# Strassen products for the gate and the first feed-forward matrix, and a feed-forward middle in quarters

## The chip, the cores and the metric

The kernel runs on one core of one Trainium2 chip. The metric is device time in microseconds (us) of one launch. TensorE (PE in the profile) multiplies, VectorE (DVE) and ScalarE (ACT) do elementwise work, GpSimd (POOL) helps with it, and SyncE (SP) issues the DMAs. TensorE's weight loads are listed apart as PEld.

## The reference

Two decoder layers over 512 tokens with 1024 features, all float32. Each layer mixes the tokens (layer 0: a gated linear recurrence and a sparse attention; layer 1: a latent attention), norms, and then runs the part that is changed here:

```
h = layer_norm(DN_ALPHA * x + m, ln1_g[i], ln1_b[i])
f = jnp.square(jax.nn.relu(h @ mlp_w1[i])) @ mlp_w2[i]
e = jax.nn.sigmoid(h @ ple_w_gate[i]) * (p[i] @ ple_w_proj[i])
x = layer_norm(DN_ALPHA * h + f + e, ln2_g[i], ln2_b[i])
```

`mlp_w1` is 1024 x 4096, `mlp_w2` 4096 x 1024, `ple_w_gate` 1024 x 1024, `ple_w_proj` 256 x 1024.

## The kernel before

Features lie on partitions, tokens along the free dimension, so an activation of 1024 features is eight tiles of 128 x 512 (`y[0]` to `y[7]` hold the residual stream). Every float32 factor is split into a high part (rounded to the matmul's format, by ScalarE) and a low part (what is left, by VectorE), and each product is three matmuls: high by high, high by low, low by high (`mm3`, lines 106 to 108).

Weights come in chunks of 1 MB (128 x 2048): 256 output features (two tiles n) by eight row tiles k. `wload` (lines 91 to 102) has SyncE fetch one into `wraw` (two buffers), ScalarE makes `whi` and VectorE `wlo` from it in two pieces of 1024 columns. `gemm_t` (lines 113 to 157) then runs 2 x 8 x 3 = 48 matmuls of 512 columns for a chunk. Where its input or its result is passed on by halves of the tokens, it runs 96 of 256 columns instead: for the first two chunks of the gate (`lead`), and for the last group of the second feed-forward matrix (`tail`).

In each layer the order is: output projection of the mixer, the first norm (class `Norm`, lines 200 to 323), `embed` (p by `w_proj`, 48 matmuls), the gate (4 chunks), and twice a half of the feed-forward part: 8 chunks of `mlp_w1` (in the text FF1), then 8 of `mlp_w2` (FF2, four groups of two chunks). The first norm works by halves of the tokens: sums over partitions by a matmul (line 255), subtraction and squares, the deviation by two more small matmuls (lines 268 and 282), then for each of the eight tiles a scaling on VectorE (line 313), the high part on ScalarE (line 321), the low part on VectorE (line 322) and the scaled residual on GpSimd (line 323). The gate's first two chunks start with the first half of the tokens while the second half is still being normed.

The order of the instructions on each engine is decided by a scheduler when the program is built, by priorities and by the buffers that are free; each engine then runs its list strictly in that order and waits on semaphores. A helper raises the priority of a weight's splitting by `ahead`. Matmul results go to 8 PSUM banks, of which six are taken in turn outside the attention.

Products are called 1 to 7 by their place in the changed code below; the names in the changed program are `xb` (the seven combined activations), `ws` (sums of weight blocks), `w..hi`/`w..lo` (their high and low parts), `u` and `c` (partial results), `n_t` and `n_h` (the norm's temporaries).

Of the kernel before, what the change touches and what calls it, by code (L numbers as in the profile page):

```python
# [52 lines left out]
def hybrid_kernel(ctx: ExitStack, tc: tile.TileContext, a: dict, out: bass.AP):  # L53
# [37 lines left out]
    def wload(dram, idx, n=2048, pieces=2, sub=None, raw=None, ahead=30):  # L91
        """A chunk of a weight (n columns), as high and low parts."""
        hi = wp.tile([P, 2048], F32R, tag="whi", name=nm("whi"))
        lo = wp.tile([P, 2048], F32R, tag="wlo", name=nm("wlo"))
# [105 lines left out]
    class Norm:  # L200
        """LayerNorm over the features (partitions and tiles) of y. The second norm of a layer
        takes mean and variance in one pass, with y centred first on the mean of tiles 0-3, so
        that the variance doesn't cancel; the first one takes the mean, then the variance."""
# [83 lines left out]
        def last(self, cs, rstd):  # L287
            """The end of the kernel: the tensor engine, free by now, takes the mean off."""
# [11 lines left out]
        def apply(self, cs):  # L300
# [111 lines left out]
    class Pair:  # L412
        """The outputs of two heads, as high and low parts in mixed[k]."""
# [14 lines left out]
    # ================= layer 0: RG-LRU and sparse attention =================  # L428
    def mixer0(mixed):
        with pool("m0", 1) as m0, pool("m0s") as sc:  # L430
# [14 lines left out]
            def key_halves(kx, kh, ps, j):  # L445
                """kx: low parts, high parts; kh: high parts on partitions 0-63."""
# [39 lines left out]
            # indexer scores of query blocks 1-3 (block 0 has no more keys than are selected)  # L486
# [21 lines left out]
            def topk():  # L508
                """16 rounds of 8, a round for all the blocks at a time."""
# [13 lines left out]
            # softplus(-lambda) by the atanh series of log1p, exact to float32  # L523
# [33 lines left out]
            # gates: sigmoid(z) = (1 + tanh(z / 2)) / 2; rg keeps the tanh, ix (1 + tanh) times  # L557
            # the convolved input
            def ev1(n, ps, cs):
# [7 lines left out]
                xh, xl = q1[:, n], q1[:, 4 + n]     # free until the queries come  # L567
# [51 lines left out]
            # distances for ALiBi beside the high parts of q and k  # L619
# [45 lines left out]
    def out_proj(dram, idxs, xs, norm, **kw):  # L665
# [8 lines left out]
        # the first two tiles in banks that the end of the attention leaves free  # L674
# [3 lines left out]
    # ================= MLP and per-layer embedding =================  # L678
    def embed(layer, mp):
        """p @ w_proj / 2, kept for the gate."""  # L680
        pr, pp = [], []
        for k in range(2):
            raw = mp.tile([P, S], F32, tag="sg", name=nm("praw"))
# [6 lines left out]
        def ev(n, ps, cs):  # L690
            t = mp.tile([P, S], F32, tag=f"ah{n + 2}", bufs=1, name=nm("pp"))
# [6 lines left out]
    def mlp(layer, h, pp, mp, norm):  # L698
        # sigmoid(z) = (1 + tanh(z / 2)) / 2
        def evg(n, ps, cs):  # L700
            sg = mp.tile([P, S], F32, tag="sg", name=nm("sg"))[:, cs]
            nc.scalar.activation(sg, ps[:, cs], AF.Tanh, scale=0.5)
            nc.vector.scalar_tensor_tensor(sg, sg, 1.0, pp[n][:, cs], op0=OP.add, op1=OP.mult)
            nc.vector.tensor_add(y[n][:, cs], y[n][:, cs], sg)

        gemm_t(a["w_gate"], [[layer * 4 + g] for g in range(4)], h, evg, lead=8, halves=("lead",))
        for half in range(2):
            act = [None] * 16

            def ev1(n, ps, cs):  # L710
                r = mp.tile([P, S], F32, tag="r", name=nm("r"))
                nc.scalar.activation(r, ps, AF.Relu)  # L712
                nc.scalar.activation(r, r, AF.Square)  # L713
# [345 lines left out]
```

## Time and profile before

| | us |
|---|---|
| median of 3 runs | 1299.29 |
| lowest, highest | 1299.01, 1301.18 |
| span of the profiled execution, first to last instruction | 1298.1 |
| TensorE busy in the span | 1254.7 |
| VectorE busy | 740.1 |
| ScalarE busy | 575.7 |
| GpSimd busy | 212.1 |

The profile is of one execution. The time of a run also counts what lies around the span; the median of the runs stands 1.2 us above the span of the profiled execution, whose own run time is not listed apart. A matmul's time in the profile is its latency, longer than its place in the stream: how fast TensorE goes is read from one start to the next. The two feed-forward stages lie at about 282 to 635 us (layer 0) and 933 to 1286 us (layer 1).

### The profile page before, as it was taken

What the parts mean: (1) busy time and instruction counts of PE and PEld (TensorE: products, weight loads), DVE (VectorE), ACT (ScalarE), POOL (GpSimd) and SP (SyncE); (2) the same over time, 40 slices, a digit from 0 to 9 for tenths busy, and PEclk for the clock granted to TensorE, in tenths of its full rate; (3) what the DMA queues carried; (4) which work ended last, traced back from release to release, by engine and by line L of the source; (5) the groups of instructions that cost most, each with busy time, mean ns of one, the idle gap of its engine ahead of it and who ended that gap; (6) DMA issues with size and microseconds to landing.
All of it is one profiled execution on the core that took longest, in us unless ns stands there. A gap on an engine that the chain in (4) does not pass through costs nothing.

```text
span 1298.1 us, 16201 instructions
## 1 busy us (share of the span) xinstructions
PE 1254.7 (97%) x6248; PEld 1049.7 (81%) x6248; DVE 740.1 (57%) x1437; ACT 575.7 (44%) x1066; POOL 212.1 (16%) x237
## 2 busy tenths in 40 slices
PE   7997889999999999999899999999999999999998
PEld 5685678988888888888887788799888888888888
DVE  5799978854432244336728898677544322344264
ACT  4465775533321133313356998635333211333132
POOL 1457550300000000000543443103000000000000
PEclk9798899999999999999898999999999999999999
DMA  6211120132222222222112100122322222222211
GB/s 212 97 66 65 66 81 34 66 130 97 98 98 97 98 98 97 97 97 86 49 65 98 33 33 28 55 77 87 127 98 97 98 95 95 92 96 94 98 49 66
DMA packets 20910, 110.81 MB, mean 85 GB/s; under 512 B 2464, under 2 KB 6560, under 8 KB 8640
## 3 DMA queue, kind: packets, MB, share of 16 engines
q1 hardware_dynamic: 20736, 109.18, 24.8%
q8 instruction: 49, 0.80, 0.3%
q0 software_dynamic: 96, 0.59, 0.2%
q14 instruction: 29, 0.24, 0.1%
HBM read 107.66 MB, written 2.10 MB: 85 GB/s over the span
## 4 chain that ended last, share of the span: by engine, by line
PE 81%; DVE 11%; ACT 6%; issue 1%; DMA 0%; POOL 0%; SPq 0%; ACTq 0%; DVEq 0%; POOLq 0%
PE ps L108 24%; PE ps L106 24%; PE ps L107 24%; ACT l L357 2%; DVE mb L517 2%; DVE m L516 1%; PE ps L370 1%; PE ps L751 1%; PE ps L749 1%; PE ps L750 1%; ACT whi L88 1%; DVE l L352 1%; PE ps L390 1%; DVE wlo L89 1%; DVE hl L322 1%
## 5 line engine op out<-in xcount | busy, mean ns | idle before, releaser
L88 ACT CAST whi<-wraw 128x1024 fp32r<-128x1024 f32 (+3 forms) x226 | 205.3, 936 | 399.3 <-PE ps L107 389.3
L106 PE MATMUL ps<-hh,whi 128*128 128x512 f32 (+1 forms) x1008 | 372.0, 371 | 10.3 <-ACT hh L88 6.6
L108 PE MATMUL ps<-hh,wlo 128*128 128x512 f32 (+1 forms) x1008 | 370.8, 370 | 7.9 <-POOL wlo L89 6.0
L107 PE MATMUL ps<-hl,whi 128*128 128x512 f32 (+1 forms) x1008 | 371.9, 370 | 1.2 <-POOL hl L89 1.2
L89 DVE TENSOR_TENSOR wlo<-wraw,whi 128x1024 fp32r<-128x1024 f32 (+1 forms) x172 | 194.1, 1147 | 250.0 <-ACT whi L88 249.9
L106 PEld LDWEIGHTS ps<-hh,whi 128*128 128x128 f32 x1008 | 191.7, 191 | 44.0 <-ACT hh L88 7.2
L108 PEld LDWEIGHTS ps<-hh,wlo 128*128 128x128 f32 x1008 | 191.4, 190 | 40.4 <-POOL wlo L89 6.7
L107 PEld LDWEIGHTS ps<-hl,whi 128*128 128x128 f32 x1008 | 192.0, 191 | 34.3 <-POOL hl L89 2.9
L107 PE MATMUL ps<-al,whi 128*128 128x512 f32 (+1 forms) x576 | 211.3, 367 | 0.0
L106 PE MATMUL ps<-ah,whi 128*128 128x512 f32 (+1 forms) x576 | 211.1, 367 | 0.0
L108 PE MATMUL ps<-ah,wlo 128*128 128x512 f32 (+1 forms) x576 | 210.5, 365 | 0.0
L107 PEld LDWEIGHTS ps<-al,whi 128*128 128x128 f32 x576 | 108.6, 189 | 17.9 <-issue 0.5
L108 PEld LDWEIGHTS ps<-ah,wlo 128*128 128x128 f32 x576 | 108.6, 189 | 17.9 <-issue 0.5
L106 PEld LDWEIGHTS ps<-ah,whi 128*128 128x128 f32 x576 | 108.6, 189 | 17.6
L323 POOL TENSOR_SCALAR y<-y,small 128x256 f32<-128x256 f32 x48 | 32.0, 678 | 492.1 <-DVE hl L322 492.1
L89 POOL TENSOR_TENSOR wlo<-wraw,whi 128x512 fp32r<-128x512 f32 (+2 forms) x54 | 91.8, 1718 | 79.1 <-ACT whi L88 79.1
L723 DVE TENSOR_TENSOR y<-y,ps 128x512 f32<-128x512 f32 (+1 forms) x36 | 22.6, 627 | 107.2 <-PE ps L108 107.2
L712 ACT ACTIVATE r<-ps 128x512 f32<-128x512 f32 x64 | 38.0, 594 | 88.0 <-PE ps L108 88.0
L361 POOL TENSOR_SCALAR l<-l,sums 128x512 f32<-128x512 f32 (+1 forms) x96 | 53.8, 578 | 98.8 <-DVE sums L359 69.6
L88 DVE CAST ah<-r 128x512 fp32r<-128x512 f32 x64 | 27.1, 423 | 71.9 <-ACT r L713 71.9
L357 ACT ACTIVATE l<-l,mx 128x512 f32<-128x512 f32 (+1 forms) x96 | 52.9, 553 | 11.8 <-DVE mx L355 11.3
L89 DVE TENSOR_TENSOR al<-r,ah 128x512 fp32r<-128x512 f32 x64 | 44.3, 693 | 2.2
(289 smaller groups left out, 1575.4 us busy)
## 6 DMA issues: line engine op xcount, KB each, us to landing
wraw<-in_mlp_w SPq DMA_DIRECT2D x64, 1024.0 KB, 4.8
wraw<-in_w_out SPq DMA_DIRECT2D x8, 1024.0 KB, 4.8
wraw<-in_w_gate SPq DMA_DIRECT2D x8, 1024.0 KB, 6.2
wraw<-in_w_in SPq DMA_DIRECT2D x6, 1024.0 KB, 4.8
wraw<-in_w_ukv SPq DMA_DIRECT2D x4, 1024.0 KB, 4.7
wraw<-in_w_in SPq DMA_DIRECT2D x16, 128.0 KB, 4.0
y<-in_xT SPq DMA_DIRECT2D x8, 256.0 KB, 4.2
wraw<-in_w_proj SPq DMA_DIRECT2D x2, 1024.0 KB, 5.8
```

Source lines behind the costliest of these rows:

```text
L88: (act or nc.scalar.copy)(hi, src)
L89: (sub or nc.vector.tensor_sub)(lo, src, f(hi))
L106: nc.tensor.matmul(ps, whi, xhi, start=start, stop=False)
L107: nc.tensor.matmul(ps, whi, xlo, start=False, stop=False)
L108: nc.tensor.matmul(ps, wlo, xhi, start=False, stop=stop)
L322: nc.vector.scalar_tensor_tensor(lo, yk, b, f(hi), op0=OP.add, op1=OP.subtract)
L323: nc.gpsimd.tensor_scalar(yk, yk, b, ALPHA, op0=OP.add, op1=OP.mult)
L357: nc.scalar.activation(L[blk], L[blk], AF.Exp, bias=mx[:, NB + blk:NB + blk + 1], scale=self.scale, accum_out=sums[:, blk:blk + 1])
L361: nc.gpsimd.tensor_scalar(L[blk], L[blk], sums[:, blk:blk + 1], 1.0, op0=OP.mult, op1=OP.mult)
L517: nc.vector.match_replace(out=w, in_to_replace=m8, in_values=src, imm_value=LOWEST)
L712: nc.scalar.activation(r, ps, AF.Relu)
L723: nc.vector.tensor_add(y[n][:, cs], y[n][:, cs], ps[:, cs])
```

## The change

The gate and FF1 take a chunk of weights as a 2 x 2 block matrix: columns in two tiles of 128, rows in two halves of four tiles. The normed activation is a 2 x 2 block matrix too: features in two halves of four tiles, tokens in two halves of 256. A Strassen scheme (Winograd's form) gets the four result blocks from seven block products in place of eight. Each is 4 x 3 = 12 matmuls of 256 columns.

For each chunk `front` makes the four weight sums S1 to S4 and the parts for the first four products, `back` those for the other three; the results are added up on VectorE (`u`, `c`). The first norm no longer makes high and low parts of the eight tiles; its new method `blocks` makes the seven activation blocks. Four of them (T1 to T4) need both halves of the tokens. The feed-forward part runs in four quarters of 4 + 4 chunks; the tail of FF2 is one chunk. A third pair of weight buffers is added in a pool `third`, the copy of the squared activation goes from VectorE to ScalarE, and the gate no longer starts by halves.

```diff
+        def blocks(self, cs, rstd):
...
+            for k in range(KT):
...
+                nc.vector.scalar_tensor_tensor(yk, yk, g, rstd, op0=OP.mult, op1=OP.mult)
+                if not half:
+                    put(k // 4, k % 4, yk, b)
+                elif k >= 4:
+                    put(2, k - 4, yk, b)
+                nc.scalar.activation(hk, yk, AF.Identity, bias=b)
+                nc.gpsimd.tensor_scalar(yk, hk, ALPHA, 0.0, op0=OP.mult, op1=OP.add)
+            if half:
+                for k in range(4):
...
+                    nc.vector.tensor_sub(t[0], b12, b11)
+                    nc.vector.tensor_sub(t[1], b22, t[0])
+                    nc.vector.tensor_sub(t[2], b22, b12)
+                    nc.vector.tensor_sub(t[3], b21, t[1])
+                    for i in (1, 2, 0, 3):
+                        put(3 + i, k, t[i])
...
+        def front(idx):
...
+            with tc.high_priority(120):
+                sp(t, 0, Q, a11)
+                nc.vector.tensor_add(s1, a21, a22)
+                nc.vector.tensor_sub(s2, s1, a11)
+                sp(t, Q, Q, s2)
+                nc.vector.tensor_sub(s3, a11, a21)
+                nc.vector.tensor_sub(s4, a12, s2)
+                sp(t, 2 * Q, 2 * Q, st[:, Q:3 * Q])
+            return t, raw, s4
...
+        def back(raw, s4):
...
+                sp(t, 0, 2 * Q, raw[:, 2 * Q:])
+                sp(t, 2 * Q, Q, s4)
...
+        for g, idx in enumerate(idxs):
+            x, raw, s4 = front(idx)
+            a = ps_tile()
+            product(a, x, 0, 0)
...
+            nc.scalar.copy(p1, a[:, :H])
+            b = ps_tile()
+            product(b, x, 4, Q)
...
+            nc.vector.tensor_add(u, b[:, :H], p1)
+            c = ps_tile()
+            product(c, x, 5, 2 * Q)
...
+            nc.vector.tensor_add(u3, c[:, :H], u)
+            d = ps_tile()
+            product(d, x, 3, 3 * Q)
...
+            nc.vector.tensor_add(t[:, 3 * H:], d[:, :H], u3)
+            w2 = back(raw, s4)
+            product(a, w2, 1, 0, 2 * P, False)
+            product(c, w2, 6, P, 2 * P, False)
+            nc.vector.tensor_add(t[:, 2 * H:3 * H], c[:, :H], u)
+            product(d, w2, 2, 2 * Q, start=False)
+            nc.vector.tensor_add(t[:, H:2 * H], d[:, :H], u)
+            evac(g, a[:, :H], t)
...
-        gemm_t(a["w_gate"], [[layer * 4 + g] for g in range(4)], h, evg, lead=8, halves=("lead",))
-        for half in range(2):
...
+        seven(a["w_gate"], [layer * 4 + g for g in range(4)], xb, mp, evg, third=third)
+        for part in range(4):
...
+            seven(a["mlp_w1"], [layer * 16 + part * 4 + g for g in range(4)], xb, mp, ev1, third=third)
...
-            gemm_t(a["mlp_w2"], [[b + 2 * g, b + 2 * g + 1] for g in range(4)], act, ev2, tail=half)
...
+            gemm_t(a["mlp_w2"], [[b + 2 * g] for g in range(4)], act, ev2, tail=part == 3)
```

How the program's lists change is shown at three places. On TensorE in layer 0, around the statistics of the second half of the tokens (line 255 before; lines 269 and 283 of the changed kernel), before:

```order
L106 MATMUL ps_2295<-hh_2003,whi_2275 128x256
L106 MATMUL ps_2299<-hh_1997,whi_2283 128x256
L255 MATMUL ps_2104<-n_s_326_1880,cst 128x256
L107 MATMUL ps_2299<-hl_1998,whi_2283 128x256
L106 MATMUL ps_2303<-hh_1997,whi_2283 128x256
L107 MATMUL ps_2303<-hl_1998,whi_2283 128x256
L107 MATMUL ps_2295<-hl_2004,whi_2275 128x256
L108 MATMUL ps_2295<-hh_2003,wlo_2276 128x256
L106 MATMUL ps_2291<-hh_2009,whi_2275 128x256
```

and of the changed kernel (`xb_2005` and `xb_2029` to `xb_2041` are blocks of the first half of the tokens, `xb_2199` and `xb_2202` the first tiles of T2 and T3; a row with x2 is two matmuls):

```order
L269 MATMUL ps_2144<-cst,n_s_327_1881 128x1 x2
L283 MATMUL ps_2152<-cst,n_d_2148 128x128 x2
L786 MATMUL ps_2510<-xb_2005,wh_2497 128x256
L786 MATMUL ps_2385<-xb_2029,whi_2445 128x256 x2
L786 MATMUL ps_2385<-xb_2029,wlo_2446 128x256
L786 MATMUL ps_2385<-xb_2035,whi_2445 128x256 x2
L786 MATMUL ps_2385<-xb_2035,wlo_2446 128x256
L786 MATMUL ps_2385<-xb_2041,whi_2445 128x256 x2
L786 MATMUL ps_2385<-xb_2041,wlo_2446 128x256
L786 MATMUL ps_2400<-xb_2199,whi_2372 128x256 x2
L786 MATMUL ps_2415<-xb_2202,whi_2372 128x256
L786 MATMUL ps_2400<-xb_2199,wlo_2373 128x256
```

Before, the gate's matmuls with the first half of the tokens stand around the statistics and behind them; in the changed list 12 + 1 + 9 matmuls of the gate need the first half alone (12 of them stand ahead of line 269), and the next ones read T2 and T3.

On VectorE in layer 0, at the end of the second half's norm, before (line 322 makes low parts of the normed tiles, lines 703 and 704 take up the gate's results):

```order
L322 SCALAR_TENSOR_TENSOR hl_2028<-y_72,small,hh_2027 128x256
L322 SCALAR_TENSOR_TENSOR hl_2034<-y_73,small,hh_2033 128x256
L313 SCALAR_TENSOR_TENSOR y_74<-y_74,small,ps_2144 128x256
L703 SCALAR_TENSOR_TENSOR sg_2382<-sg_2382,pp_2206 128x256
L703 SCALAR_TENSOR_TENSOR sg_2389<-sg_2389,pp_2215 128x256
L322 SCALAR_TENSOR_TENSOR hl_2040<-y_74,small,hh_2039 128x256
L704 TENSOR_TENSOR y_67<-y_67,sg_2382 128x256
```

and of the changed kernel (lines 357 to 364 make T1 to T4, line 342 their low parts, lines 765 to 769 the weight sums of the gate's first chunk, line 752 low parts of weights):

```order
L364 TENSOR_TENSOR n_t_410_2254<-n_h_354_2003,n_t_408_2252 128x256
L342 TENSOR_TENSOR xb_2259<-n_t_408_2252,xb_2259 128x256
L342 TENSOR_TENSOR xb_2262<-n_t_409_2253,xb_2262 128x256
L342 TENSOR_TENSOR xb_2268<-n_t_410_2254,xb_2268 128x256
L765 TENSOR_TENSOR ws_2374<-wraw_2370 128x512
L768 TENSOR_TENSOR ws_2374<-wraw_2370 128x512
L766 TENSOR_TENSOR ws_2374<-ws_2374,wraw_2370 128x512
L752 TENSOR_TENSOR wl_2498<-wraw_2495,wh_2497 128x512
L769 TENSOR_TENSOR ws_2374<-wraw_2370,ws_2374 128x512
L752 TENSOR_TENSOR wlo_2373<-ws_2374,whi_2372 128x512
L752 TENSOR_TENSOR wlo_2373<-ws_2374,whi_2372 128x1024
```

All sixteen T tiles and their low parts stand ahead of the first weight sum, and the low part of S2, which the second product reads, is the sixth behind the last T.

On VectorE in a chunk of FF1, before (low parts of the next chunk's weights, two copies and two low parts of the activation for each chunk):

```order
L89 TENSOR_TENSOR wlo_2872<-wraw_2873,whi_2871 128x1024 x2
L88 CAST ah_2795<-r_2792 128x512
L89 TENSOR_TENSOR al_2796<-r_2792,ah_2795 128x512
L88 CAST ah_2835<-r_2832 128x512
L89 TENSOR_TENSOR al_2836<-r_2832,ah_2835 128x512
```

and of the changed kernel (lines 809, 813 and 815 add up results of one chunk, the others prepare weights of later ones):

```order
L809 TENSOR_TENSOR c_3703<-ps_3690,u_597_3688 128x256
L752 TENSOR_TENSOR wlo_3836<-wraw_3760,whi_3835 128x1024
L752 TENSOR_TENSOR wlo_3836<-ws_3764,whi_3835 128x512
L765 TENSOR_TENSOR ws_3894<-wraw_3890 128x512
L813 TENSOR_TENSOR c_3703<-ps_3675,u_595_3673 128x256
L766 TENSOR_TENSOR ws_3894<-ws_3894,wraw_3890 128x512
L768 TENSOR_TENSOR ws_3894<-wraw_3890 128x512
L752 TENSOR_TENSOR wl_3893<-wraw_3890,wh_3892 128x512
L752 TENSOR_TENSOR wl_3893<-ws_3894,wh_3892 128x512
L769 TENSOR_TENSOR ws_3894<-wraw_3890,ws_3894 128x512
L752 TENSOR_TENSOR wl_3893<-ws_3894,wh_3892 128x1024
L815 TENSOR_TENSOR c_3703<-ps_3690,u_595_3673 128x256
```

VectorE's list for a chunk grows from six instructions to sixteen, and additions that free a PSUM bank stand between the preparations of later weights.

## Rows read from the trace of the kernel before

**Rows 1.** The page: span, busy time of the engines, chain of waits by engine.

```profile
span 1298.1 us, 16201 instructions
...
PE 1254.7 (97%) x6248; PEld 1049.7 (81%) x6248; DVE 740.1 (57%) x1437; ACT 575.7 (44%) x1066; POOL 212.1 (16%) x237
...
PE 81%; DVE 11%; ACT 6%; issue 1%; DMA 0%; POOL 0%; SPq 0%; ACTq 0%; DVEq 0%; POOLq 0%
```

**Rows 2.** Windows, a feed-forward stretch: busy us of PE, PEld, DVE, ACT, POOL, clock.

```profile
300.00:400.00 100.00, 100.00 (x443) 82.81 (x442) 38.10 (x48) 32.47 (x44) 0.00 (x0) 1.00 0.29 98
```

**Rows 3.** Timeline, PE: start, us, operation; widths 512, then 256.

```profile
600.00 0.39 PE L106 MATMUL ps<-ah,whi 128*128 128x512 f32 x1
...
608.84 0.39 PE L106 MATMUL ps<-ah,whi 128*128 128x512 f32 x1
...
609.52 0.28 PE L106 MATMUL ps<-ah,whi 128*128 128x256 f32 x1
...
615.88 0.28 PE L108 MATMUL ps<-ah,wlo 128*128 128x256 f32 x1
```

**Rows 4.** Instructions by line and form, DVE and ACT: count, busy us, mean ns.

```profile
L89 DVE TENSOR_TENSOR wlo<-wraw,whi 128x1024 fp32r<-128x1024 f32 x156 | 187.9, 1222 | 244.0 <-ACT whi L88 244.0
L88 ACT CAST whi<-wraw 128x1024 fp32r<-128x1024 f32 x178 | 182.7, 1048 | 391.9 <-PE ps L107 388.0 <-issue 3.8
...
L89 DVE TENSOR_TENSOR al<-r,ah 128x512 fp32r<-128x512 f32 x64 | 44.3, 693 | 2.2
L713 ACT ACTIVATE r<-r 128x512 f32<-128x512 f32 x64 | 40.4, 631 | 1.0
...
L313 DVE SCALAR_TENSOR_TENSOR y<-y,small,ps 128x256 f32<-128x256 f32 x56 | 24.1, 474 | 2.7 <-PE ps L282 2.6
...
L257 DVE TENSOR_TENSOR y<-y,ps 128x256 f32<-128x256 f32 x32 | 12.2, 412 | 0.9 <-PE ps L255 0.8
```

**Rows 5.** Timeline, DVE: instructions in a row (x is their count).

```profile
217.80 1.42 DVE L257 TENSOR_TENSOR y<-y,ps 128x256 f32<-128x256 f32 x4
...
245.55 1.26 DVE L313 SCALAR_TENSOR_TENSOR y<-y,small,ps 128x256 f32<-128x256 f32 x3 [0.80 <-PE ps L282]
...
249.10 2.74 DVE L322 SCALAR_TENSOR_TENSOR hl<-y,small,hh 128x256 fp32r<-128x256 f32 x5
...
259.72 2.36 DVE L89 TENSOR_TENSOR wlo<-wraw,whi 128x1024 fp32r<-128x1024 f32 x2
...
590.73 2.50 DVE L232 TENSOR_TENSOR y<-y,n_c 128x512 f32<-128x512 f32 x4 [0.22 <-ACT n_c L230]
```

**Rows 6.** Windows around the first norm, layers 0 and 1.

```profile
234.90:245.50 10.60, 9.61 (x78) 9.29 (x77) 8.81 (x21) 4.49 (x11) 1.43 (x2) 1.00 0.26 90
245.50:264.40 18.90, 18.50 (x135) 17.13 (x134) 15.50 (x33) 11.16 (x21) 5.42 (x8) 1.00 0.24 78
...
893.90:912.80 18.90, 18.50 (x146) 17.70 (x146) 12.59 (x28) 9.41 (x19) 5.25 (x8) 1.00 0.09 38
```

**Rows 7.** Timelines, PE: third gate chunk, both layers; DVE: norm of layer 1.

```profile
259.74 0.50 PE L106 MATMUL ps<-hh,whi 128*128 128x512 f32 x1 [0.33 <-ACT whi L88]
...
910.89 0.50 PE L106 MATMUL ps<-hh,whi 128*128 128x512 f32 x1 [0.33 <-ACT whi L88]
...
893.93 1.26 DVE L313 SCALAR_TENSOR_TENSOR y<-y,small,ps 128x256 f32<-128x256 f32 x3 [0.80 <-PE ps L282]
```

**Rows 8.** Timeline, DVE: end of layer 0, second norm.

```profile
624.59 0.42 DVE L312 TENSOR_TENSOR y<-y,ps 128x256 f32<-128x256 f32 x1 [0.41 <-PE ps L282]
...
637.15 0.41 DVE L239 TENSOR_TENSOR n_s<-n_s,y 128x256 f32<-128x256 f32 x1
...
638.46 1.49 DVE L239 TENSOR_TENSOR n_s<-n_s,y 128x256 f32<-128x256 f32 x1
```

**Rows 9.** Windows at that place.

```profile
634.90:640.00 5.10, 2.06 (x9) 1.34 (x8) 5.07 (x10) 3.69 (x8) 5.10 (x7) 1.00 0.37 116
640.00:647.00 7.00, 6.76 (x25) 5.63 (x26) 4.93 (x11) 0.94 (x3) 3.72 (x3) 0.58 0.28 87
```

More of the change, by code (lines that the diff above doesn't have):

```diff
@@ L16 @@
 S = 512
+H = S // 2
 NB = S // P
@@ L307, in apply @@
                 return
+            if not self.onepass:
+                self.blocks(cs, rstd)
+                return
             for k in range(KT):
@@ L323, in apply, with put, new_x @@
                 nc.gpsimd.tensor_scalar(yk, yk, b, ALPHA, op0=OP.add, op1=OP.mult)
+        def blocks(self, cs, rstd):
+            half = cs.start // H
+            if not half:
+                self.hf = [self.t(f"n_h{k}") for k in range(KT)]
+                self.xb = [[None] * 4 for _ in range(7)]
+            def put(j, k, src, bias=None):
+                t = self.xb[j][k] = self.new_x(j, k)
+                if bias is None:
+                    nc.scalar.copy(t[:, :H], src)
+                    nc.vector.tensor_sub(t[:, H:], src, f(t[:, :H]))
+                else:
+                    nc.scalar.activation(t[:, :H], src, AF.Identity, bias=bias)
+                    nc.vector.scalar_tensor_tensor(t[:, H:], src, bias, f(t[:, :H]), op0=OP.add, op1=OP.subtract)
+            for k in range(KT):
+                g, b = small[:, self.base + k:self.base + k + 1], small[:, self.base + 8 + k:self.base + 9 + k]
+                yk, hk = y[k][:, cs], self.hf[k][:, cs]
+                nc.vector.scalar_tensor_tensor(yk, yk, g, rstd, op0=OP.mult, op1=OP.mult)
+                if not half:
+                    put(k // 4, k % 4, yk, b)
[5 more added lines that the diff above has]
+                for k in range(4):
+                    (b11, b12), (b21, b22) = ([self.hf[i][:, c] for c in HALVES] for i in (k, k + 4))
+                    t = [self.t(f"n_t{i}", H, 2) for i in range(4)]
+                    nc.vector.tensor_sub(t[0], b12, b11)
[4 more added lines that the diff above has]
+                        put(3 + i, k, t[i])
+        def new_x(self, j, k):
+            n = 4 * j + k
+            if n < 12:
+                return self.xpool.tile([P, S], F32R, tag=f"xb{n}", bufs=1, name=nm("xb"))
+            n -= 12
+            return res.tile([P, S], F32R, tag=f"h{'hl'[n % 2]}{n // 2}", name=nm("xb"))
     S_AT = {3: ("A", 0), 2: ("B", 0), 1: ("C", 0), 0: ("C", 2 * P)}
@@ L696, in embed, with mlp, evg, ev1 @@
         return pp
[L698 to L704, printed above, removed]
[L706 to L720 removed]
+    def mlp(layer, xb, pp, mp, third, norm):
+        def evg(g, c11, t):
+            nc.scalar.activation(t[:, H:], t[:, H:], AF.Tanh, scale=0.5)
+            nc.scalar.activation(t[:, :H], c11, AF.Tanh, scale=0.5)
+            for i in range(2):
+                n, r = 2 * g + i, t[:, i * S:(i + 1) * S]
+                nc.vector.scalar_tensor_tensor(r, r, 1.0, pp[n], op0=OP.add, op1=OP.mult)
+                nc.vector.tensor_add(y[n], y[n], r)
+        seven(a["w_gate"], [layer * 4 + g for g in range(4)], xb, mp, evg, third=third)
+        for part in range(4):
+            act = []
+            def ev1(g, c11, t):
+                nc.scalar.activation(t[:, :H], c11, AF.Relu)
+                nc.scalar.activation(t[:, H:], t[:, H:], AF.Relu)
+                nc.scalar.activation(t, t, AF.Square)
+                for i in range(2):
+                    n, r = 2 * g + i, t[:, i * S:(i + 1) * S]
+                    hi = mp.tile([P, S], F32R, tag=f"ah{n}", bufs=1, name=nm("ah"))
+                    lo = mp.tile([P, S], F32R, tag=f"al{n}", bufs=1, name=nm("al"))
+                    split(hi, lo, r)
+                    act.append((hi, lo))
+            seven(a["mlp_w1"], [layer * 16 + part * 4 + g for g in range(4)], xb, mp, ev1, third=third)
@@ L722, in ev2 @@
             def ev2(n, ps, cs):
                 nc.vector.tensor_add(y[n][:, cs], y[n][:, cs], ps[:, cs])
-                if half == 1:
+                if part == 3:
                     if n == 3:
@@ L949, in hybrid_kernel @@
         with pool(f"mlp{layer}") as mp:
-            with tc.tile_pool(name=f"norm{layer}a", bufs=1) as npool:
-                norm = Norm(npool, layer, 0)
+            with pool(f"norm{layer}a", 1) as npool:
+                norm = Norm(npool, layer, 0, xpool=mp)
                 if layer == 0:
@@ L956, in hybrid_kernel @@
                 pp = embed(layer, mp)
-            with tc.tile_pool(name=f"norm{layer}b", bufs=1) as npool:
-                h, norm = norm.h, Norm(npool, layer, 1, final=layer == 1)
-                mlp(layer, h, pp, mp, norm)
+            with pool(f"norm{layer}b", 1) as npool, pool(f"third{layer}") as third:
+                xb, norm = norm.xb, Norm(npool, layer, 1, final=layer == 1)
+                mlp(layer, xb, pp, mp, third, norm)
                 h = norm.h
```

56 lines of the change are left out of this document (45 added, 11 removed).

## The prediction

> **What bounds the kernel now.** I read the page first. TensorE is busy 1254.7 of 1298.1 us, and the chain that ended last runs 81% of the span over it, 11% over VectorE [rows 1]. Then the stretches: in the middle of the feed-forward part TensorE is busy 100.00 of 100 us at full clock, VectorE 38.10 and ScalarE 32.47 [rows 2]. There only fewer or cheaper matmuls give time back, and the other engines have over half of it free. Around the first norm it is still TensorE (9.61 of 10.60 us, then 18.50 of 18.90, in layer 1 18.50 of 18.90), but VectorE is busy 15.50 of the 18.90 us beside it [rows 6]: the gate's matmuls with the first half of the tokens cover the norm of the second.
>
> **Matmuls.** Starts give the price: 39 matmuls of 512 columns in 8.84 us are 0.227 us each, 53 of 256 columns in 6.36 us 0.120 us [rows 3]. Half the columns cost 53%, not 50%. A chunk before is 48 x 0.227 = 10.88 us, after 7 x 12 = 84 x 0.120 = 10.08 us: 0.80 us less, 7% and not the 12.5% of the product count. 32 chunks of FF1 give 25.6 us; in each layer's shorter tail 96 of 256 columns (11.5 us) become 48 of 512 (10.9), 1.3 us in all. The gate is counted with the norm below.
>
> The Trainium skill (TensorE: Matmul & The Clock Gate, Back-to-back issue gap) gives columns / 2.4 GHz plus 2.5 ns for a lone matmul's place in the stream, and for a full-size one in a stream with weight loads even less. By that a chunk would fall from 10.36 to 9.17 us, 1.19 us instead of 0.80, and the sum would come out some 15 us lower over 40 chunks. The rows above disagree with the figures (0.227 and 0.120 us, not 0.216 and 0.109), so the sum keeps the rows.
>
> **The norm, the largest term.** Before, the second half's scaling starts at 245.55 us in layer 0 [rows 5] and 893.93 in layer 1 [rows 7]; call it X. The lists show what TensorE still has then: 22 matmuls of the gate in layer 0 and 12 in layer 1 need the first half alone, then all needs T2 and the split S2. On VectorE behind X stand 8 scalings at 0.395 us ((1.26 - 0.47) / 2), 4 low parts at 0.55 (2.74 / 5) and 16 + 16 subtractions of 256 columns at 0.337 ((1.42 - 0.41) / 3) [rows 4, 5]: 3.2 + 2.2 + 10.8 = 16.1 us. Then come S1, S3, S2 at 0.60 each ((2.50 - 0.69) / 3; blocks of 512, the strides as yet unpriced). ScalarE takes first the 1024 columns of S3 and S1, 1.05 us, then S2, 0.63 by the activation of that size [rows 4]; the former can start when S3 is there, 17.3 us behind X. So TensorE resumes at X + 19.0, 264.6 and 912.9 us. VectorE's own path to the low part of S2, 16.1 + 6 x 0.60 = 19.7, ends beside it.
>
> From there the gate has 314 matmuls left (324 in layer 1): 37.7 and 38.9 us, so it ends at 302.2 and 951.8. Before, its last two chunks start at 259.74 and 910.89 [rows 7] and end 21.8 us later, 281.5 and 932.7. The shift is 20.7 + 19.2 = 39.9 us, the cheaper gate included. I take no shift of X itself: before, weight splitting of the gate is on VectorE in that stretch too, in larger pieces. Bounds: 4 us earlier a layer if the two chains overlap better, 4 later below.
>
> **GpSimd beside that chain.** With GpSimd busy throughout (5.10 of 5.10 us [rows 9]), an addition of two SBUF operands took 1.49 us [rows 8], against 0.41 for the same form just before it, and low parts took 0.55 instead of the 0.47 of a scaling. `blocks` issues eight GpSimd scalings in that stretch, some four of them beside the T subtractions. At that row's loss of 1.08 us four cost 4.3 us a layer, at the 0.08 of the low parts next to nothing; I take 2 us a layer, 4 in all (0 to 8.6).
>
> The skill (SBUF — State Buffer, section SBUF: two separate sides) says that VectorE with two SBUF inputs and a GpSimd instruction that reads SBUF lock one another out for a whole instruction. That speaks against this change: nearly all T steps have two SBUF inputs, where the old norm's scaling reads PSUM. The 1.49 us agree; with the full loss beside all eight the term would be 8.6 us a layer instead of 2.
>
> **Clock.** Behind 3 us without matmuls at the end of layer 0 the granted clock fell: 0.58 of full over 7 us, so most of it at 1.2 of 2.4 GHz [rows 9], worth 7 x 0.42 = 2.9 us. The new hole is some 19 us behind X, longer than that, so the restart pays this, partly while VectorE is late anyway: 2 us a layer, 4 (0 to 6).
>
> **VectorE as second bound.** A chunk of FF1 now costs it 4 sums x 0.60, 3 low parts of 512 x 0.60, 2 of 1024 x 1.14 (2.36 - 1.22), 5 additions x 0.337 and 2 low parts of the activation x 0.60: 2.4 + 1.8 + 2.3 + 1.7 + 1.2 = 9.4 us of TensorE's 10.08; a chunk of the gate (four steps of 512 in place of two) 10.6 us [rows 4, 5]. That is by starts with nothing waited for; by full durations (0.69, 1.22, 0.41) it is 10.7 and 12.1. Gate and first quarter of FF1 stand back to back: VectorE 80.0 us against TensorE's 78.0, both without slack, and VectorE begins them late, coming from the norm. I take 5 us a layer, 10 (0 to 13 a layer). In the three later quarters the preceding FF2 lets VectorE prepare about a chunk and a half ahead, as the third buffer pair allows; 24 chunks, 5 us in all (0 to 16). The copy moved to ScalarE costs nothing: its chunk is 2 casts of 1024 and a square (1.05 each), five casts of 512 (0.63 each) and, as estimates between these and below, 0.8 for a relu and 0.4 twice: 7.9 us beside 10.08.
>
> **FF1 to FF2.** FF2 now starts with eight tiles, not sixteen, and the last two come from one chunk: addition 0.41, relu and square of some 0.8 and 1.05, cast 0.63, low part 0.69, about 3.9 us with a matmul's latency, and weight casts of 1.05 in between in the first quarter. TensorE has 18 matmuls of cover, 4.1 us. Eight such places at 0 to 1.5: 5 us.
>
> **Shorter tail.** FF2's last group runs 5.8 us a half instead of 11.5. In layer 0 VectorE works on the first half's norm from 624.59 until the second half's sums at 637.15 [rows 8], already behind TensorE; with 5.8 us less cover this comes later by about that: 5 us (0 to 8). At the kernel's end there is no low part to make: 3 us (0 to 6).
>
> **Sum.** 39.9 - 25.6 - 1.3 + 4 + 4 + 10 + 5 + 5 + 8 = +49 us on a span of 1298.1, 1347; the median stands 1.2 us above the span: 1348 us. All small terms at zero, 1312; all at their upper ends, about 1394.
>
> **Rivals.**
> - The hole alone counts, VectorE keeps up and the small terms stay near zero: 1312 to 1322. For it: VectorE's 60% of free time in the feed-forward part. Against: 93% of the pace in FF1, over 100% in the gate. Chance 0.13.
> - VectorE sets the pace of the whole gate and FF1, by durations rather than starts: 10.7 us for 10.08 in 32 chunks, 12.1 in 8: 1375 to 1394. For it: results and weights cross between three engines, so it will wait often. Chance 0.17.
> - Faster: the hole closes because TensorE gets T2 early. Break-even without small terms is 13 us less in two holes, a resumption at X + 12.5; at X + 9 (no more than scalings and low parts, as before) the time would be about 1292. For it: only if VectorE or ScalarE ran the T steps at half the price. Against: the lists, which are fixed. Chance 0.05.
> - A balance within 0.2% (2.6 us, what a measurement of this kernel can tell): 0.03.
> - My forecast, 1325 to 1375: 0.62.
>
> So slower 0.92, same 0.03, faster 0.05; the range 1312 to 1390 leaves out about 0.14: both of these and the edges of the first two rivals.
>
> **What would show it.** Right: TensorE idle over 20 us behind each first norm's second statistics, ended by T2 or S2's parts; 256-column starts 0.120 us apart; FF2 unchanged at 10.88 a chunk; VectorE busy over 85% in gate and FF1. Wrong: TensorE at work within 12 us of X, 256-column starts well under 0.120, or FF1 chunks at 11 us with VectorE idle between instructions.

## The result, and the profile after

The changed kernel takes 1318.36 us (median of 4 runs, 1316.99 to 1319.66), the kernel before beside it 1300.07 (1299.01 to 1301.18): 1.0141 times as long, 95% interval 1.0127 to 1.0155, 18.3 us slower. The forecast had the sign, and 1318 is inside 1312 to 1390, but its +49 us is over twice what was measured. The profiled execution has a span of 1317.8 us, 19.7 above that of before.

The page of the changed kernel, the lines that answer to [rows 1]:

```profile
span 1317.8 us, 19322 instructions
...
PE 1228.2 (93%) x7400; PEld 1083.4 (82%) x7400; DVE 989.8 (75%) x1925; ACT 702.3 (53%) x1306; POOL 205.1 (16%) x237
...
PE 74%; DVE 16%; ACT 7%; issue 2%; DMA 0%; POOL 0%; ACTq 0%; SPq 0%; DVEq 0%; POOLq 0%
```

TensorE is busy 26.5 us less, VectorE 250 us more, and the span is longer all the same: TensorE has idle time that it did not have. Where, the windows tell (busy us of PE, PEld, DVE, ACT, POOL, then granted clock): first from the end of layer 0's embed product to the norm's second statistics, then the hole, the restart, the rest of the gate, the first quarter, a later quarter of FF1, and the hole of layer 1.

```profile
221.50:243.60 22.10, 16.07 (x79) 13.32 (x78) 18.58 (x50) 16.17 (x39) 3.84 (x8) 0.91 0.00 0
243.60:260.90 17.30, 0.50 (x4) 0.21 (x2) 16.79 (x46) 11.44 (x30) 3.33 (x8) 0.50 0.00 0
260.90:280.00 19.10, 19.10 (x137) 19.05 (x138) 17.53 (x28) 11.31 (x17) 0.00 (x0) 0.84 0.33 111
280.00:304.50 24.50, 24.16 (x202) 23.75 (x201) 24.17 (x41) 10.96 (x19) 0.00 (x0) 1.00 0.37 124
304.50:344.80 40.30, 39.49 (x325) 38.82 (x325) 37.51 (x65) 23.87 (x37) 0.00 (x0) 1.00 0.30 105
388.00:428.50 40.50, 40.50 (x340) 40.38 (x339) 33.68 (x53) 25.73 (x39) 0.00 (x0) 1.00 0.31 105
903.00:921.20 18.20, 0.71 (x5) 0.52 (x5) 17.47 (x47) 12.13 (x31) 3.34 (x8) 0.56 0.00 0
```

Where before had TensorE busy 18.50 of 18.90 us [rows 6], it now stands idle 16.8 of 17.3 us in layer 0, with another 6.0 of the 22.1 us ahead of them, and 17.5 of 18.2 in layer 1. In the first quarter of FF1 it loses 0.8 of 40.3 us, in a later one nothing, beside a VectorE that is busy 83% of it and no longer 38% [rows 2]. With the windows cut to line 786 alone, the three later quarters of layer 0:

```profile
388.40:428.50 40.10, 39.97 (x336) 40.06 (x336) 1.00 0.32 106
471.95:512.35 40.40, 40.23 (x336) 40.25 (x336) 1.00 0.31 105
555.90:596.05 40.15, 40.01 (x336) 40.09 (x336) 1.00 0.31 106
```

Four chunks in 40.0 to 40.2 us are 10.0 us a chunk, 0.119 us a matmul: the saving against 10.88 arrives in full. The hole in detail, VectorE from the second half's first scaling (X of the forecast, 245.55 before [rows 5]), then ScalarE, then TensorE (brackets: idle time before, and what ended it):

```profile
244.11 2.83 DVE L350 SCALAR_TENSOR_TENSOR y<-y,small,ps 128x256 f32<-128x256 f32 x7 [1.31 <-PE ps L283]
...
250.70 1.42 DVE L342 TENSOR_TENSOR xb<-n_t,xb 128x256 fp32r<-128x256 f32 x4
...
259.08 1.08 DVE L342 TENSOR_TENSOR xb<-n_t,xb 128x256 fp32r<-128x256 f32 x3
260.09 0.68 DVE L765 TENSOR_TENSOR ws<-wraw 128x512 f32<-128x512 f32 x1
...
261.29 0.68 DVE L766 TENSOR_TENSOR ws<-ws,wraw 128x512 f32<-128x512 f32 x1
```

```profile
259.19 0.41 ACT L341 CAST xb<-n_t 128x256 fp32r<-128x256 f32 x1 [0.27 <-DVE n_t L364]
260.20 0.62 ACT L751 CAST wh<-wraw 128x512 fp32r<-128x512 f32 x1 [0.60 <-DVE xb L342]
```

```profile
242.85 1.22 PE L283 MATMUL ps<-cst,n_d 128*128 128x128 f32 x4 [0.69 <-DVE n_d L278]
260.87 0.58 PE L786 MATMUL ps<-xb,wh 128*128 128x256 f32 x1 [16.80 <-ACT wh L751]
...
263.01 0.41 PE L786 MATMUL ps<-xb,wlo 128*128 128x256 f32 x1
263.23 0.84 PE L786 MATMUL ps<-xb,whi 128*128 128x256 f32 x3
...
266.13 0.41 PE L786 MATMUL ps<-xb,whi 128*128 128x256 f32 x1
266.35 0.41 PE L786 MATMUL ps<-xb,wlo 128*128 128x256 f32 x1
266.56 0.54 PE L786 MATMUL ps<-xb,whi 128*128 128x256 f32 x2
```

VectorE needs 15.98 us from X to the first weight sum (forecast 16.1). TensorE starts again at 260.87 with ten matmuls that need the first half alone. They stand in its queue behind the first of them, whose weight cast ScalarE reaches only after its last T cast (260.20). The first matmul with T2 and S2 is the one at 263.23, X + 19.1 (forecast X + 19.0). In layer 1 X is 903.73 and that matmul 922.13, X + 18.4. Up to 266.56 most starts are 0.213 us apart, at the lower level of the clock, then 0.120.

Account of the spans, each piece against the kernel before. By its starts, that kernel ends the gate at 281.99 and 933.14; the places to compare with, 4 and 28 chunks later, are 325.51 and 586.63 in layer 0, 976.66 and 1237.78 in layer 1. Layer 1 is counted less the 13.2 us by which it starts late. Of the forecast's terms for VectorE in the later quarters and for the changes from FF1 to FF2 each piece has its share.

| piece | forecast | measured |
|---|---|---|
| layer 0: hole, gate, first quarter (FF2 starts at 344.86, before 325.51) | +27.1 | +19.4 |
| layer 0: to the FF2 of the last quarter (596.07, before 586.63) | -5.2 | -9.9 |
| layer 0: tail and boundary, to the same matmul of layer 1 (848.70, before 835.54) | +4.4 | +3.7 |
| layer 1: hole, gate, first quarter (FF2 at 1004.07) | +25.6 | +14.2 |
| layer 1: to the FF2 of the last quarter (1255.45) | -5.2 | -9.7 |
| layer 1: tail and end | +2.4 | +2.0 |
| sum | +49 | +19.7 |

### The profile page after: what moved, and what is told of

It reads as the page before. It is cut to its first block, busy times and chain, and to the rows that moved or that the text cites. A ratio compares the mean times of both kernels' runs of the same rounds, so it can differ in the third digit from the quotient of the medians.

```text
span 1317.8 us, 19322 instructions
## 1 busy us (share of the span) xinstructions
PE 1228.2 (93%) x7400; PEld 1083.4 (82%) x7400; DVE 989.8 (75%) x1925; ACT 702.3 (53%) x1306; POOL 205.1 (16%) x237
## 4 chain that ended last, share of the span: by engine, by line
PE 74%; DVE 16%; ACT 7%; issue 2%; DMA 0%; POOL 0%; ACTq 0%; SPq 0%; DVEq 0%; POOLq 0%
PE ps L786 29%; PE ps L107 12%; PE ps L108 12%; PE ps L109 12%; ACT l L408 2%; DVE mb L568 1%; DVE m L567 1%; PE ps L421 1%; DVE xb L342 1%; PE ps L897 1%; ACT whi L89 1%; PE ps L898 1%; PE ps L896 1%; DVE n_s L252 1%; DVE wlo L752 1%
## 5 line engine op out<-in xcount | busy, mean ns | idle before, releaser
L786 PE MATMUL ps<-xb,whi 128*128 128x256 f32 x1512 | 279.1, 286 | 0.2 <-ACT whi L751 0.2
L786 PEld LDWEIGHTS ps<-xb,whi 128*128 128x128 f32 x1512 | 239.4, 194 | 1.6 <-ACT whi L751 0.4
L786 PE MATMUL ps<-xb,wlo 128*128 128x256 f32 x756 | 215.0, 286 | 1.2 <-DVE wlo L752 1.2
L786 PE MATMUL ps<-xb,wh 128*128 128x256 f32 x728 | 131.7, 282 | 34.3 <-ACT u L797 17.5
L786 PEld LDWEIGHTS ps<-xb,wlo 128*128 128x128 f32 x756 | 146.4, 194 | 2.2 <-DVE wlo L752 2.2
L786 PEld LDWEIGHTS ps<-xb,wh 128*128 128x128 f32 x728 | 111.9, 190 | 35.4 <-ACT u L797 17.7
L107 PE MATMUL ps<-hh,whi 128*128 128x512 f32 (+1 forms) x304 | 112.7, 373 | 8.9 <-ACT hh L89 5.8
L109 PE MATMUL ps<-hh,wlo 128*128 128x512 f32 (+1 forms) x304 | 111.4, 369 | 6.7 <-POOL wlo L90 6.0
L108 PE MATMUL ps<-hl,whi 128*128 128x512 f32 (+1 forms) x304 | 112.8, 371 | 1.8 <-POOL hl L90 1.8
L107 PEld LDWEIGHTS ps<-hh,whi 128*128 128x128 f32 x304 | 59.4, 196 | 19.4 <-ACT hh L89 6.4
```

The source lines that it names most:

```text
L107: nc.tensor.matmul(ps, whi, xhi, start=start, stop=False)
L108: nc.tensor.matmul(ps, whi, xlo, start=False, stop=False)
L109: nc.tensor.matmul(ps, wlo, xhi, start=False, stop=stop)
L786: nc.tensor.matmul(o, u[:, c], v, start=start and k == n == 0, stop=k == 3 and n == 2, skip_group_check=True)
```

## The experiments

The theory after this reading (H): the hole behind the first norm is the whole loss, and it is VectorE's chain of T steps; the seven products save in full. Against it: VectorE is also full in FF1 (V), or the hole is made by queue order and memory (Q). All times below are medians, the ratios to the kernel before beside them.

**1. The gate plain, FF1 by seven products.** The blocks of the first three products are halves of the h tiles; the T's are made behind the gate's code, and the second norm's temporaries use the memory of the blocks.

```
-        seven(a["w_gate"], ..., xb, mp, evg, third=third)
+        gemm_t(a["w_gate"], ..., h, evg, lead=8, halves=("lead",))
+                gate(layer, norm.h, pp, npool)
+                xb = norm.ts()          # T1 to T4, now after the gate's code
```

> The gate goes back to eight block products in before's order (first half of the tokens first), so that its matmuls lie beside the norm of the second half; only FF1 keeps the seven products, its T blocks are made beside the gate. Theory H (the hole behind the first norm is the whole loss, the seven products save in full): no shift at the gate's end, 16 FF1 chunks a layer at 0.85 us less = -13.6 a layer, +3.4 at the layer boundary, +1.9 at the end: 1278 us (1274 to 1284). Rival V (VectorE has no room for the T steps beside the gate and the first quarter): up to 12 us a layer come back as waits of the first quarter's matmuls, 1290 to 1302.

1293.07 us, 0.9947 (0.9930 to 0.9963). The hole is gone (TensorE 13.00 of 13.00 us from 247 to 260) and the kernel faster than before, but 15 us short of H, at V's near end. V's reason does not fit the place, though; windows ahead of and in the first quarter, layer 0 and 1:

```profile
275.00:285.00 10.00, 10.00 (x51) 8.39 (x49) 3.71 (x8) 2.50 (x5) 0.00 (x0) 1.00 0.01 2
285.00:300.00 15.00, 12.36 (x89) 12.09 (x89) 13.78 (x21) 6.57 (x12) 0.00 (x0) 0.89 0.19 70
931.00:945.00 14.00, 10.04 (x70) 9.41 (x69) 11.05 (x18) 6.30 (x10) 0.00 (x0) 0.88 0.23 75
```

VectorE is idle 6.3 of the 10 us before TensorE starves. Its list there:

```profile
279.67 0.69 DVE L843 TENSOR_TENSOR y<-y,sg 128x512 f32<-128x512 f32 x1
284.59 1.23 DVE L749 TENSOR_TENSOR wlo<-wraw,whi 128x1024 fp32r<-128x1024 f32 x1 [4.23 <-ACT whi L748]
285.73 0.69 DVE L842 SCALAR_TENSOR_TENSOR sg<-sg,pp 128x512 f32<-128x512 f32 x1
286.53 0.69 DVE L843 TENSOR_TENSOR y<-y,sg 128x512 f32<-128x512 f32 x1
287.13 0.69 DVE L762 TENSOR_TENSOR ws<-wraw 128x512 f32<-128x512 f32 x1
```

The first weight sum of FF1 (`ws`) stands right behind the last read of the gate's scratch tile `sg`. Two causes could do that: `ws` was given the memory that `sg` leaves, or the second weight pair waited for a buffer that the gate holds (the 4.23 us for a cast). Experiments 5, 9 and 10 part them.

**2. Quarters without the seven products.**

```
-        for half in range(2):                     # 8 + 8 chunks
+        for part in range(4):                     # 4 + 4 chunks
-            gemm_t(a["mlp_w2"], [[b + 2 * g, b + 2 * g + 1] for g in range(4)], act, ev2, tail=half)
+            gemm_t(a["mlp_w2"], [[b + 2 * g] for g in range(4)], act, ev2, tail=part == 3)
```

> The kernel before with the feed-forward middle in quarters and the shorter tail, no seven products. Theory H: the six more changes between FF1 and FF2 cost nothing, the shorter tail 3.4 us at the layer boundary and 1.9 at the end: 1305 us (1302 to 1308). The forecast's terms (5 for the changes between FF1 and FF2, 8 for the tail, -1.3): 1312. Third: nothing at all, 1300.

1303.05 us, 1.0027 (1.0018 to 1.0037): +3.3, inside H's range. The forecast's +12 for this part of the change was too much.

**3. A longer tail in the changed kernel.**

```
-            gemm_t(a["mlp_w2"], ..., act, ev2, tail=part == 3)
+            gemm_t(a["mlp_w2"], ..., act, ev2, tail=2 * (part == 3))
```

> The changed kernel with two chunks of FF2 by halves of the tokens at the end of each layer, not one. If the shorter tail costs what the traces show (3.4 us at the layer boundary, 1.9 at the end): 1313 us. If those 5.3 us come from elsewhere (pools, order of the second norm): 1318 to 1320, the 1.3 us dearer matmuls included.

1315.69 us, 1.0124 (1.0109 to 1.0139): 2.7 less than the changed kernel, with intervals that overlap; half of the 5.3. In the traces the stretch from the last quarter's FF2 to layer 1 falls from 252.6 to 249.6 us (595.50 to 845.10), the one to the end by 1.1. The wait for the norm's sums does not go: it was 2.96 us in the middle of the tail and is now behind it,

```profile
654.15 0.34 PE L269 MATMUL ps<-cst,n_s 128*128 128x1 f32 x1 [4.53 <-DVE n_s L240]
```

**4. The T steps left out.**

```
                 for k in range(4):
+                    for i in range(4):
+                        self.xb[3 + i][k] = self.xb[(2, 1, 2, 0)[i]][k]
+                    continue
```

> The changed kernel without the T steps: T1 to T4, their casts and low parts are left out, and the blocks of the tokens stand in their place. Theory H (VectorE's chain of 32 T steps, 10.8 us, sets the hole's end): TensorE resumes 8 to 9 us behind X instead of 17 to 19, 10 to 11 us less in each layer, some of it plus 1 us for the clock: 1296 us (1293 to 1300). Rival Q (TensorE's queue or the memory of the third weight pair, shared with the norm's tiles, sets it): under 4 us a layer, 1311 or more.

1297.12 us, 0.9981 (0.9971 to 0.9990): 21.2 us less than the changed kernel, 10.6 a layer. The hole's end:

```profile
249.06 0.58 PE L789 MATMUL ps<-xb,wh 128*128 128x256 f32 x1 [6.01 <-ACT wh L754]
```

6.01 us of idle time where there were 16.80: the difference, 10.8 us, is what 32 steps at 0.337 us come to. Q as it was priced (under 4 us a layer) falls: the T chain on VectorE makes two thirds of the hole. Why TensorE can't take the T's one by one while they are made is another question; experiment 8 comes back to it.

**5. Plain gate, and nothing shared with it** (both edits on top of the first experiment).

```
-                gate(layer, norm.h, pp, npool)
+                gate(layer, norm.h, pp, mp)       # sg in memory of its own
     def mlp(layer, xb, pp, mp, third, norm):
+        wn[0] = 1                                 # chunk 0: first pair ordinary, second pair third
```

> As the first experiment (plain gate, seven products for FF1 alone), which came to 1293 us because TensorE waits some 15 us in all in the first quarters, and VectorE stands idle 6.5 of the 10 us before the first of them. Here the gate's scratch tile no longer shares memory with the weight sums of FF1, and the first chunk's second weight pair goes to the third buffer, which the gate doesn't hold. Theory M (the sums waited for memory, not for VectorE): most of the 15 us go, 1279 to 1286 us. Theory V (VectorE itself is full there): 1290 or more.

1282.27 us, 0.9867 (0.9853 to 0.9882): inside the range of theory M, 17.4 us faster than before. It is also inside H's range for the first experiment (1274 to 1284), worked out with the same tail.

**6. The same with the longer tail**: the edit of experiment 3 on top of experiment 5.

> The same with two chunks of FF2 by halves at the end of each layer. The tail of two alone took 2.7 us off the changed kernel, so 2 to 4 us under the run beside it: 1276 to 1284.

1277.39 us, 0.9833 (0.9816 to 0.9849): 22.2 us faster than before, 41.0 faster than the changed kernel. The longer tail takes off 4.9 us here, more than the 2 to 4 expected. FF2 of the first quarter starts at 323.14 us, where the kernel before has 325.51.

**7. More work for VectorE in FF1.**

```
+                for _ in range(1 + again[0]):     # 4 in the three later quarters, else 0
                     nc.vector.tensor_add(s1, a21, a22)
```

> The changed kernel, but in the three later quarters of each layer the sum S1 of every weight chunk is made five times over: four more VectorE steps of 0.60 us in each of 24 chunks, 2.4 us a chunk on top of 9.4, where TensorE needs 10.03. If VectorE sets the pace of FF1: 24 x 1.8 = 42 us more, 1361. If the buffers let it work ahead beside FF2, as the trace of the changed kernel suggests (FF1 quarters of 39.9 us, no wait): a debt of 7 us a quarter, under the 15 us that it can be ahead: 1318 to 1322 us. Half of it ahead: 1335 to 1345.

1327.84 us, 1.0218 (1.0203 to 1.0233): 9.5 us for 57.6 us of added work, between the first two numbers and near the lower. The windows of three quarters of FF1 and the FF2 between the last two:

```profile
387.70:427.80 40.10, 40.10 (x337) 40.05 (x336) 35.42 (x58) 24.65 (x38) 0.00 (x0) 1.00 0.26 83
...
471.50:515.80 44.30, 41.54 (x338) 40.54 (x337) 40.75 (x67) 24.99 (x38) 0.00 (x0) 1.00 0.28 96
515.80:559.20 43.40, 43.40 (x194) 35.97 (x193) 28.58 (x39) 13.07 (x16) 0.00 (x0) 1.00 0.36 121
559.20:599.50 40.30, 40.30 (x339) 40.15 (x338) 35.59 (x59) 24.01 (x37) 0.00 (x0) 1.00 0.25 81
```

Only one of the three (in layer 1 too) is late, by some 3 us. In the others VectorE is busy 35.42 and 35.59 of 40 us, where the changed kernel has 33.29 and 30.69, although it has 9.6 us more to do: the rest is done ahead, beside FF2, where VectorE has 28.58 of 43.40 us, and had 23.51 in the changed kernel:

```profile
515.80:559.20 43.40, 43.40 (x205) 36.22 (x204) 23.51 (x31) 11.66 (x16) 0.00 (x0) 1.00 0.30 98
```

**8. The weight sums left out.**

```
-                nc.vector.tensor_add(s1, a21, a22)
-                nc.vector.tensor_sub(s2, s1, a11)
-                sp(t, Q, Q, s2)
-                nc.vector.tensor_sub(s3, a11, a21)
-                nc.vector.tensor_sub(s4, a12, s2)
-                sp(t, 2 * Q, 2 * Q, st[:, Q:3 * Q])
+                sp(t, Q, Q, a21)
+                sp(t, 2 * Q, 2 * Q, raw[:, Q:3 * Q])
```

> The changed kernel without the four weight sums of any chunk: S1 to S4 are left out, and the casts read blocks of the raw weights. VectorE then has 7 us of work for a chunk of FF1 instead of 9.4. If VectorE costs only what waits the trace shows in the gate and the first quarter (about 2 us a layer) and the sums stand in the hole (S3, S1, S2 before the second product, 1.8 us, and what the cast of S2 waits, about 3 us in all): 4 to 5 us a layer, 1308 to 1311 us. If the pace of VectorE costs 5 us a layer there and 5 in the later quarters, as forecast: 1297 to 1303. If nothing of it is on the path: 1317.

1307.88 us, 1.0067 (1.0052 to 1.0082): 10.5 less, just beyond the first case. In the traces 4.0 and 3.7 us of it lie before the FF2 of the first quarter (340.90 in layer 0), and the later quarters are what they were (39.9 to 40.0 us). So 2.4 us a chunk taken from VectorE buys nothing there, and in the gate and first quarter it buys some 4 us a layer, with what the sums cost inside the hole; the two were not parted.

The trace shows one thing more about the hole. Here TensorE restarts at 251.46 us, 5.8 us behind its X (245.70), though all the T's are still made:

```profile
251.46 0.58 PE L780 MATMUL ps<-xb,whi 128*128 128x256 f32 x1 [5.80 <-ACT xb L341]
...
263.52 1.02 PE L780 MATMUL ps<-xb,wh 128*128 128x256 f32 x4 [1.54 <-ACT wh L751]
```

It takes the T tiles as they come and is busy 9.66 of 12.10 us from 251.40 to 263.50, at a granted clock of 0.59. So the hole of the changed kernel needs both: the T chain, and the weight sums standing behind it. The sums' pool opens where that of the first norm closes, so shared memory could be what holds them back, as it does in experiment 1; no run tried that in the changed kernel. From X to FF2 of the first quarter experiment 8 takes 95.2 us, the changed kernel 100.75, although TensorE restarts 11 us closer to X: an earlier restart gives back only part of the idle time.

**9 and 10. One edit each of experiment 5**: the memory of `sg`, and the buffer of the second weight pair.

> The first experiment (plain gate, seven products for FF1) with only one of the two edits that took it from 1293 to 1282 us: the gate's scratch tile moved out of the memory that the weight sums reuse. If the shared memory made the sums late: 1283 to 1286 us. If it was the gate's hold on the second weight buffer: 1290 to 1293.

> The other edit alone: the second weight pair of FF1's first chunk goes to the third buffer, the scratch tile stays where it was. The reverse: 1290 to 1293 us if the memory was the cause, 1283 to 1286 if the buffer was. Half and half: 1286 to 1289 for both.

1282.99 us (0.9863, 0.9846 to 0.9879) and 1293.55 us (0.9937, 0.9915 to 0.9959). It is the memory: experiment 9 comes within 0.7 us of experiment 5, experiment 10 stays where experiment 1 was. The wait for the cast is still 3.79 us in experiment 10, so its edit did little; that the buffer costs nothing rests on experiment 9, which leaves it as it was. With `sg` elsewhere the first sum stands at 277.35, behind the last T, 10 us earlier:

```profile
276.01 1.42 DVE L360 TENSOR_TENSOR xb<-n_t,xb 128x256 fp32r<-128x256 f32 x4
277.35 0.68 DVE L762 TENSOR_TENSOR ws<-wraw 128x512 f32<-128x512 f32 x1
```

and TensorE is busy 15.00 of the 15 us from 285 to 300 where it had 12.36.

**11. Quarters and the longer tail, no seven products**: the kernel of experiment 2 with the edit of 3.

> The kernel before in quarters with two chunks of FF2 by halves at the end of each layer, no seven products: beside the sixth experiment it differs by the seven products of FF1 and their T blocks alone. The quarters cost nothing and the tail is then as long as before, so 1300 us (1298 to 1302); the seven products of FF1 are then worth 20 to 25 us of the 27 that 32 chunks at 0.85 give. If quarters have a cost of their own beside the tail's: 1303.

1302.15 us, 1.0016 (1.0007 to 1.0026), just outside the 1298 to 1302 expected. Beside experiment 6 the seven products of FF1 are worth 24.8 us, 91% of 32 x 0.85, together with what goes with them: their T's, the third weight pair and the copy moved to ScalarE, which no run took apart. In the trace the quarters themselves cost nothing: of 2.4 us of longer span 0.7 lie ahead of the first norm, where the two programs do the same, 0.6 around the layer boundary and 1.0 behind the start of the last quarter's FF2 in layer 1. The cause of these stays open.

## Why the prediction was right in its sign and wrong in its size

- **Matmuls.** Right: 0.119 us by starts, 10.0 us a chunk where 10.08 was forecast. Taking the pitch from the rows, not the half of 512 columns, was what made this term hold.
- **The norm's hole.** Right as a mechanism and in its length (16.0 us of VectorE for 16.1, X + 19.1 and X + 18.4 for X + 19.0), shown by experiment 4 and, from the other side, by 1; that the weight sums behind the T's are part of it, as the forecast had it, experiment 8 shows. Wrong in one point: "I take no shift of X itself". X came 1.4 us earlier in layer 0 and 3.4 in layer 1 (903.73 less the late start of 13.2 is 890.6, before 893.93 [rows 7]). That is 4.8 of the 29.3 us too many. Two readings were off with little effect: 12 of the 22 matmuls of layer 0 that TensorE "still has then" had run before X, and the gate of the kernel before ends at 281.99 and 933.14, not 281.5 and 932.7, 1 us in all.
- **GpSimd beside that chain.** 4 us forecast, 1.0 measured. The last of the eight GpSimd scalings ends at 250.5 us, and behind it every T subtraction takes 0.34 us by starts. Beside the scalings VectorE steps with two SBUF inputs do get longer, 0.52 and 0.61 us where they take 0.48 (low parts) or 0.41 (subtractions) alone: 0.5 us in each layer. VectorE, then GpSimd:

```profile
248.42 0.61 DVE L345 SCALAR_TENSOR_TENSOR xb<-y,small,xb 128x256 fp32r<-128x256 f32 x1
...
250.16 0.61 DVE L364 TENSOR_TENSOR n_t<-n_h,n_t 128x256 f32<-128x256 f32 x1
```

```profile
248.32 0.44 POOL L356 TENSOR_SCALAR y<-n_h 128x256 f32<-128x256 f32 x1 [0.42 <-ACT xb L344]
...
250.06 0.45 POOL L356 TENSOR_SCALAR y<-n_h 128x256 f32<-128x256 f32 x1 [0.43 <-DVE xb L345]
```

  Both steps end 0.27 us behind the scaling that ran when they started, as do the other two of layer 0 and the four of layer 1. The rule of the Trainium skill (SBUF — State Buffer, SBUF: two separate sides), that GpSimd and a VectorE step with two SBUF inputs lock one another out, agrees with these ends. So the loss is about what is left of the GpSimd instruction, and the forecast's price of 1.08 us came from a place where these are long: beside the step of 1.49 us [rows 8] the kernel before has

```profile
638.41 1.26 POOL L89 TENSOR_TENSOR wlo<-wraw,whi 128x512 fp32r<-128x512 f32 x1
```

  In `blocks` they are 0.44 us, and only one T step has to wait for one.
- **Clock.** 2 us a layer forecast; from the starts 27 matmuls at 0.213 us (256 columns at 1.2 GHz) instead of 0.120 in layer 0, 2.5 us, and 18 in layer 1, 1.7.
- **VectorE as second bound.** This is the step that failed. It charged 10 us in gate and first quarter and 5 in the later ones, from VectorE's 93% of TensorE's pace. Measured are 2.7 us and nothing. The waits, for low parts:

```profile
300.70 0.38 PE L786 MATMUL ps<-xb,wl 128*128 128x256 f32 x1 [0.34 <-DVE wl L752]
...
323.38 0.39 PE L786 MATMUL ps<-xb,wlo 128*128 128x256 f32 x1 [0.81 <-DVE wlo L752]
...
971.16 0.38 PE L786 MATMUL ps<-xb,wl 128*128 128x256 f32 x1 [0.63 <-DVE wl L752]
```

  Ahead of these three the starts are 0.63, 1.09 and 0.91 us apart where 0.119 is the pitch; with three smaller gaps that makes 1.6 us in layer 0 and 1.1 in layer 1. In the six later quarters there is none. For gate and first quarter the forecast's own sum by starts, VectorE 80.0 us against 78.0, gives 2 us a layer and is near this; the rest of the 5 had no row behind it. For the later quarters experiment 7 shows why: added load that exceeds the pace by 1.8 us a chunk, 42 us in all, cost 9.5, because most of it is worked off beside FF2. A share of busy time within FF1 is no price. How much of that room the third weight pair gives, which the forecast named, no run shows.
- **FF1 to FF2.** 5 us forecast, no wait found: the first matmul of FF2 starts 0.12 us behind the last product's in all eight quarters (428.46 to 428.58 in the second).
- **Tail.** 8 us forecast less 1.3 for cheaper matmuls, 6.7; 3.7 + 2.0 = 5.7 measured in the changed kernel. The longer tail took 2.7 us off the changed kernel, 4.9 off experiment 5 and 0.9 off experiment 2: the order of size is confirmed, the number is not.

Of the 29.3 us too many, 19 lie up to the first FF2 of each layer, 9 in the later quarters, 1 in tail and end. By terms, VectorE as second bound makes 12 of them, FF1 to FF2 5, X 4.8, GpSimd 3, the 0.07 us that each of 40 chunks came cheaper some 3, the tail and the end of the gate before 1 each. The time that came about is that of the forecast's first rival (the hole alone counts, VectorE keeps up, 1312 to 1322), which had a chance of 0.13. That it is met has some luck in it: the clock and the tail did not stay near zero, and the earlier X and the cheaper matmuls took off about as much. Most small terms had been put above zero and none below; added up they were the error.

Of the forecast's own signs of being right, the starts (0.119 us) and FF2 (no wait) came as described; the idle stretch stayed under 20 us (16.8 and 17.5), and VectorE's share in the later quarters just under 85% (83% in the one shown).

## What to carry over

A saving on the bounding engine holds only while something covers the work that prepares it: here the seven products lose 18 us with the gate among them, and win 17 with the same tail (22 with the longer one) where a plain gate covers the T steps and the weight sums have memory of their own. When an engine is near its bound in one stage and has slack in the next, first ask how far the buffers let it work ahead, and only then charge it by its busy share. And where two pools take turns in the same memory, look for a first write that stands right behind another tile's last read: that is a wait that no engine's load explains, and here it cost 10 us.

## What the runs showed of the hardware that was not expected

Nothing new of a kind, three sizes. At the restart after 17 us with almost no matmul, with a granted clock of 0.50 in the hole of layer 0, most starts stay at 0.213 us for 5.7 us in layer 0 and 4.4 in layer 1. A VectorE step of 256 columns with two SBUF inputs that starts beside a GpSimd instruction ends 0.27 us behind it, whether that takes 0.44 us, as here, or 1.26 us, as at the end of layer 0 before (0.28 us there). And TensorE takes 256-column matmuls at 0.119 us over 336 in a row with a new weight for each (40.06 us of weight loads beside 39.97 of matmuls), 52% of the 0.227 for 512 columns.
